# Gates of the forgetting branch ahead of its projections, and the output projection of two row blocks taken channel by channel behind the merges

## The chip, the cores and the metric

The kernel runs on one core of one Trainium2 chip. A core has TensorE (PE) for matrix products, VectorE (DVE), ScalarE (ACT) and GpSimd (POOL) for elementwise work, and SyncE (SP), whose queue issues nearly all the transfers here. The metric is the device time of one execution in microseconds; times given are medians of several runs. A profile is one execution taken by the hardware profiler. In it "PEld" is TensorE's loading of the stationary operand, which overlaps its products, and "L109" is line 109 of the kernel.

## What is computed

One decoder layer over 512 positions (T) of 1024 channels (D), in float32. An input u = x * (1 + scale) + shift is projected by one matrix into queries, keys and values of two attention branches of 8 heads each, into forget logits, and into two gates of 1024 channels. The part that the change touches is this, cut from the reference:

```
merged = jax.nn.sigmoid(g_a) * (y_fox @ w_fox_proj) + jax.nn.sigmoid(g_b) * (y_sb @ w_sb_proj)
attn_out = merged @ w_o
x = _layer_norm(DEEPNORM_ALPHA * x + (1.0 + gt1) * attn_out, ln1_g, ln1_b)
u2 = x * (1.0 + sc2) + sh2
h = _causal_depthwise_conv(u2 @ w_up, conv_w, conv_b)
```

g_a is the gate of the forgetting branch (FoX), g_b that of the stick-breaking branch. Behind it comes a gated MLP of width 2816 with its own layer norm.

## The kernel before

**Precision.** Each float32 operand is split into a high and a low part (names end in h and l: `hi_of` on ScalarE, `lo_of` on VectorE, line 77), and a product is three matmuls: high by high, high by low, low by high (`mm3`, lines 109 to 111). A matmul reads 128 rows against up to 512 columns.

**Weights.** All weight tiles (128 x 1024, 512 KB) stand in one list, `items`, in the order in which they are added. `weights(i, ahead)` issues the loads on SP's queue (line 125), up to item i + 3, into four buffers `raw`, and calls the processing of items up to i + `ahead` (2 unless said otherwise). `split_proc` splits a tile into `wh` and `wl`, three buffers of each. `ada_proc` turns a tile of the modulation matrix into one column of shift or scale (`mod_col`) on VectorE. `wo_proc` (line 573) multiplies a tile of w_o by (1 + gate), `gt[0]`, on GpSimd, then splits it in two halves into `woh` and `wol`, which stay in the pool `z` of 60 buffers.

**Order.** SP's queue keeps the order in which the program is written. On the other engines a scheduler orders the instructions: by its own model of their durations it issues what is ready, the one written first ahead of the others; on the chip each engine then works through its queue in that fixed order. The work that fills TensorE between the steps of the heads is a list, `stream`, of generators: projections of q, k and the gates (`proj`, 24 matmuls each), of the branches' outputs (`bproj`, 12 matmuls each). `fill(n)` takes n matmuls from it. Behind the last head `fill(1 << 30)` empties it.

**The merge.** `bproj(0, j)` multiplies the forgetting branch's output by columns j of its projection; VectorE multiplies the product by the sigmoid of gate j (line 568); `merge(j)` adds the other branch's share `ma[j]` on GpSimd (line 674) and splits the sum into `mh[j]` (ScalarE) and `ml[j]` (VectorE). `mh` and `ml` hold channels 128 j to 128 j + 127 of `merged`, transposed. j runs over the eight channel tiles (KT = 8).

In the list the order behind the heads is: `bproj(0, 0)`, a w_o tile, gate 3, `bproj(0, 1)`, a w_o tile, gate 4, and so on to gate 7; then `bproj` 5, 6 and 7; then the last three w_o tiles.

**The output projection.** `o_main(i)` (line 807) computes 128 rows of attn_out, in two halves e of 512 columns: 8 channels x 2 halves x 3 matmuls = 48, lines 817 to 819, into two PSUM banks (of eight). Then VectorE adds the residual `xn` (a load of x, line 813; add at 822) and normalizes (`ln_stats`). `o_turn(i)` transposes the block (line 836, eight transposes), scales it (lines 839 and 840) and splits it into `u2h` and `u2l`. The first three tiles of the up-projection (NSPLIT = 3) are multiplied with blocks 0 and 1 first (`up_mm` with 256 columns), then with blocks 2 and 3:

```
weights(last_wo, 0)
o_main(0)
o_main(1)
o_turn(0)
o_main(2)
o_turn(1)
o_main(3)
o_turn(2)
```

Of the kernel before, what the change touches and what calls it, by code (L numbers as in the profile page):

```python
# [8 lines left out]
F32 = mybir.dt.float32  # L9
# [7 lines left out]
P = 128  # L17
T = 512
D = 1024
KT = D // P  # L20
# [24 lines left out]
def layer_kernel(ctx: ExitStack, tc: tile.TileContext, out, xT, x, cT, crow, wa0, wa1, bcol, bgt, w1, wct, wv, bf,  # L45
                 wp, wo, lncol, lnrow, wup, cwb, wdn):
    nc = tc.nc
    ctx.enter_context(tc.manual_schedule(engines={nc.sync.engine}))
    V, S, G, PE = nc.vector, nc.scalar, nc.gpsimd, nc.tensor
# [10 lines left out]
    def nm(s):  # L60
        cnt[0] += 1
        return f"{s}_{cnt[0]}"

    def bank():
        return pp.tile([P, 512], F32, name=nm("ps"), tag="ps")
# [7 lines left out]
    def hi_of(o, i, scale=1.0):  # L73
        S.activation(o, i, AF.Copy, scale=scale)  # L74

    def lo_of(o, i, hi):
        return V.tensor_tensor(o, i, fl(hi), ALU.subtract)  # L77
# [27 lines left out]
    def z(dt, s, shape=(P, 512)):  # L105
        return zp.tile(list(shape), dt, name=nm(s), tag="z", bufs=NZ)
# [10 lines left out]
    def add_item(src, proc, cols=1024):  # L117
        items.append([src, proc, cols, None, None])
        return len(items) - 1

    def weights(i, ahead=AHEAD):
        while state["load"] < min(len(items), i + LOADS):
            it = items[state["load"]]
            it[3] = stg.tile([P, 1024], F32, name=nm("raw"), tag="raw", bufs=LOADS)
            nc.sync.dma_start(it[3][:, 0 : it[2]], it[0])
            state["load"] += 1
            while state["proc"] <= state["load"] - LOADS:
                process()
        while state["proc"] < min(len(items), i + 1 + ahead):
            process()  # L130
        return items[i][4]

    def process():
        it = items[state["proc"]]
        if state["proc"] < EARLY:
            with tc.issue_after(state["after"].ins):
                it[4] = it[1](it[3])
        else:
            it[4] = it[1](it[3])
        state["proc"] += 1  # L140
# [374 lines left out]
    def ada_proc(n):  # L515
        def f(r):
            if 8 <= n < 24:
                mod_col(2 + (n - 8) // 8, n % 8, r)
                return
            g, q = n // 4, n % 4  # L520
            if q == 0:
                ada_st[g] = z(F32, "ac2")
                V.tensor_scalar_mul(ada_st[g], r[:, 0:512], cTs[:, 0:1])
            acc = ada_st[g]
            for e in range(2):
                k = 2 * q + e
                if k > 0:
                    V.scalar_tensor_tensor(acc, r[:, e * 512 : (e + 1) * 512], cTs[:, k : k + 1], acc, ALU.mult, ALU.add)
        return f
# [24 lines left out]
    def gate_after(br, j):  # L554
        def f(ps):
            sg[(br, j)] = z(F32, "sg")
            S.activation(sg[(br, j)], ps, AF.Sigmoid)
        return f
# [12 lines left out]
    woh, wol = [], []  # L571
# [27 lines left out]
    stream, sums = [], []  # L599
    adas = [0]  # L600

    skip = [4]

    def add_ada(n=1):
        for _ in range(n):
            if skip[0]:
                skip[0] -= 1
            elif adas[0] < 24:
                add_item(wa1[adas[0]], ada_proc(adas[0]))
                adas[0] += 1  # L610
                if adas[0] in (4, 8):
                    stream.append((ada_split, (adas[0] // 4 - 1, len(items) - 1)))
                    sums.append([len(stream) + 1, adas[0] // 4 - 1])
# [4 lines left out]
    def add_proj(n, after):  # L618
        stream.append((proj, (add_item(wct[TILES.index(n)], split_proc), after)))
        flush_sum(len(stream))  # L620

    def flush_sum(n):
        if sums and n >= sums[0][0]:
            stream.append((ada_sum, (sums.pop(0)[1],)))
# [3 lines left out]
    def add_bproj(br, j, after):  # L628
        if j % 2 == 0:
            wpi[br] = add_item(wp[br, j // 2], split_proc)  # L630
        stream.append((bproj, (br, j, wpi[br], after)))
# [16 lines left out]
    def add_gate(br, j):  # L648
        add_proj(("sb" if br == 1 else "fox", j), gate_after(br, j))
        add_ada()  # L650
# [12 lines left out]
    for p in (5, 6, 7):  # L663
        add_pair(p)
        for _ in range(3):
            if bj:
                j = bj.pop(0)
                add_bproj(1, j, lambda m, j=j: ma.__setitem__(j, m))

    mh, ml = [], []  # L670

    def merge(j):
        def f(m):
            G.tensor_tensor(m, m, ma[j], ALU.add)
            a, b = z(F32R, "mh"), z(F32R, "ml")
            hi_of(a, m)
            lo_of(b, m, a)
            mh.append(a)
            ml.append(b)
        return f  # L680

    wos = [0]

    def add_wo():
        if wos[0] < KT:
            add_item(wo[wos[0]], wo_proc)
            wos[0] += 1

    for j in range(3):
        add_gate(0, j)  # L690
    marks["y0"] = len(stream)
    flush_sum(1 << 30)
    for j in range(KT):
        add_bproj(0, j, merge(j))
        if j < 5:
            add_wo()
        if j + 3 < KT:
            add_gate(0, j + 3)
    skip[0] = 0
    add_ada(24 - adas[0])  # L700
    while wos[0] < KT:
        add_wo()
    last_wo = len(items) - 1

    cur = {"n": 0, "g": None}
# [76 lines left out]
    def ln_stats(st):  # L782
        mv = cons.tile([P, 8], F32, name=nm("mv"), tag="mv", bufs=2)
        V.bn_aggr(mv[:, 0:2], st)
        v, s, y, t = mv[:, 2:3], mv[:, 3:4], mv[:, 4:5], mv[:, 5:6]
        S.activation(s, mv[:, 1:2], AF.Sqrt, bias=epsc)
        V.tensor_scalar_add(v, mv[:, 1:2], EPS)
        V.reciprocal(y, s)
        V.scalar_tensor_tensor(t, y, y, v, ALU.mult, ALU.mult)
        V.scalar_tensor_tensor(y, t, -3.0, y, ALU.add, ALU.mult)  # L790
        return mv[:, 0:1], y
# [13 lines left out]
    lnr = []  # L805

    def o_main(i):
        tb = slice(i * P, (i + 1) * P)
        xn = [z(F32, "xn") for _ in range(2)]
        st = cons.tile([P, 2, 6], F32, name=nm("st"), tag="st", bufs=2)  # L810
        ps2 = [bank(), bank()]
        for e in range(2):
            nc.sync.dma_start(xn[e], x[tb, e * 512 : (e + 1) * 512])
        cut = 6 if i == 0 else KT
        for e, ks in ((0, range(cut)), (1, range(cut)), (0, range(cut, KT)), (1, range(cut, KT))):
            for k in ks:
                PE.matmul(ps2[e], mh[k][:, tb], woh[k][e], start=k == 0, stop=False)  # L817
                PE.matmul(ps2[e], mh[k][:, tb], wol[k][e], start=False, stop=False)  # L818
                PE.matmul(ps2[e], ml[k][:, tb], woh[k][e], start=False, stop=k == KT - 1)  # L819
        for e in range(2):  # L820
            ps = ps2[e]
            V.scalar_tensor_tensor(xn[e], xn[e], ALPHA, ps, ALU.mult, ALU.add)
            V.bn_stats(st[:, e, :], xn[e])
        mu, rs = ln_stats(st)
        for e in range(2):
            V.tensor_scalar(xn[e], xn[e], mu, rs, ALU.subtract, ALU.mult)
        x1.append(xn)

    def o_turn(i):
        tb = slice(i * P, (i + 1) * P)  # L830
        xn = x1[i]
        pts = [bank(), bank()]
        ufs = [z(F32, "uf2"), z(F32, "uf2")]
        for e in range(2):
            for q in range(4):
                PE.transpose(pts[e][:, q * P : (q + 1) * P], xn[e][:, q * P : (q + 1) * P], ident)
        for q in range(4):
            c = slice(q * P, (q + 1) * P)
            S.activation(ufs[0][:, c], pts[0][:, c], AF.Identity, bias=bm[:, q : q + 1], scale=gm[:, q : q + 1])
            V.tensor_scalar(ufs[1][:, c], pts[1][:, c], gm[:, q + 4 : q + 5], bm[:, q + 4 : q + 5], ALU.mult, ALU.add)  # L840
        for e in range(2):
            uf = ufs[e].rearrange("p (a b) -> p a b", b=P)
            hi_of(u2h[:, 4 * e : 4 * e + 4, tb], uf)
            lo_of(u2l[:, 4 * e : 4 * e + 4, tb], uf, u2h[:, 4 * e : 4 * e + 4, tb])
# [23 lines left out]

    weights(last_wo, 0)
    o_main(0)  # L870
    o_main(1)
    o_turn(0)
    o_main(2)
    o_turn(1)
    o_main(3)
    o_turn(2)
    weights(wui[0], 0)
    bks = [bank() for n in range(NSPLIT)]
# [7 lines left out]
    for n in range(2 * FT):  # L886
        if n < NSPLIT:
            h, l = items[wui[n]][4]
            ps = bks[n]
            up_mm(ps, h, l, slice(256, 512))  # L890
        else:
            ps = bank()
# [49 lines left out]
    for i in range(NB):  # L942
        tb = slice(i * P, (i + 1) * P)
# [6 lines left out]
        for n, (e, c0, c1) in enumerate(pieces):  # L950
            sole = (i, e) == own
            ps = bank()[:, 0 : c1 - c0] if sole else acc[i][e]
# [87 lines left out]
```

## Time and profile before

| what | value |
|---|---|
| time, median of 3 runs | 780.85 us (780.64 to 781.18) |
| span of the profiled execution, first to last instruction | 779.4 us |
| runs' median above that span | 1.45 us |
| instructions | 9533 |
| TensorE clock granted, mean | 0.990 |
| moved to and from memory | 99.67 MB, mean 128 GB/s |

The profiled execution has no time of its own beside the span; what lies around the span is taken from the runs. The busy time of an engine is the time in which it executes something; a row of the timeline gives start, duration, engine, line, operation, output and inputs by the program's names, and in brackets the idle time before it and what ended it. In a row of the stretches (from:to) stand the length, then the busy time and number of instructions of PE, PEld, DVE, ACT and POOL, then the granted clock of TensorE (1.00 is full speed), the share of time in which the transfer engines were busy, and GB/s.

### The profile page before, as it was taken

The page shows a single profiled execution, that of the slowest core. Times are in us where ns is not written, and L with a number is a line of the kernel's source. Part 1 is how long each engine was busy: PE and PEld are TensorE (multiplying, and loading weights), DVE is VectorE, ACT ScalarE, POOL GpSimd, SP SyncE. Part 2 cuts the span into 40 slices and gives each one's busy share as a digit, 9 for nine tenths or more (in the row PEclk, how much of TensorE's full clock was granted, in tenths as well). Part 3 has the DMA queues.
Part 4 walks back from the last instruction along what each step waited for, and adds up shares of the span by engine and source line. Part 5 has one row for each costly group of instructions (what it writes and reads, how often), then busy time and mean ns, then how long its engine had stood idle before and what let it go on. Part 6 is the DMA issues. An engine that isn't in the chain of part 4 may idle for free.

```text
span 779.4 us, 9533 instructions
## 1 busy us (share of the span) xinstructions
PE 754.0 (97%) x3556; PEld 624.5 (80%) x3556; DVE 553.8 (71%) x854; ACT 350.6 (45%) x583; POOL 145.3 (19%) x106
## 2 busy tenths in 40 slices
PE   5998999999999999997999999999999999999995
PEld 3886887888888888885889888888888888888885
DVE  5979999967677876676546887777666665534666
ACT  3357686727567564344115434444444443222300
POOL 1020002000010012363000590000000043945500
PEclk9999999999999999999899999999999999999998
DMA  8951244452332423544301524353332314332302
GB/s 312 404 190 55 82 144 148 142 181 96 112 128 85 146 89 132 172 167 154 116 1 42 204 80 162 108 185 115 124 107 91 108 54 163 108 107 82 108 27 82
DMA packets 31104, 99.67 MB, mean 128 GB/s; under 512 B 4273, under 2 KB 4785, under 8 KB 31058
## 3 DMA queue, kind: packets, MB, share of 16 engines
q1 hardware_dynamic: 30546, 99.00, 36.4%
q8 instruction: 28, 0.46, 0.3%
q0 software_dynamic: 512, 0.07, 0.1%
q14 instruction: 18, 0.15, 0.1%
HBM read 96.88 MB, written 2.10 MB: 127 GB/s over the span
## 4 chain that ended last, share of the span: by engine, by line
PE 76%; DVE 8%; ACT 6%; DMA 5%; issue 3%; POOL 2%; SPq 0%; DVEq 0%; POOLq 0%; ACTq 0%
PE ps L109 14%; PE ps L110 14%; PE ps L111 14%; PE ps L253 6%; PE ps L932 5%; PE ps L931 5%; PE ps L933 5%; PE ps L817 2%; PE ps L494 2%; PE ps L476 2%; PE ps L818 2%; DMA raw<-in_wa 2%; PE ps L819 2%; ACT wh L74 1%; PE ps L419 1%
## 5 line engine op out<-in xcount | busy, mean ns | idle before, releaser
L77 DVE TENSOR_TENSOR wl<-raw,wh 128x1024 fp32r<-128x1024 f32 (+2 forms) x106 | 146.0, 1377 | 96.6 <-ACT wh L74 95.9
L74 ACT ACTIVATE wh<-raw 128x1024 fp32r<-128x1024 f32 (+2 forms) x106 | 110.3, 1041 | 109.1 <-PE ps L933 38.4
L109 PE MATMUL ps<-u2h,wh 128*128 128x512 f32 (+1 forms) x376 | 141.4, 376 | 0.0
L110 PE MATMUL ps<-u2l,wh 128*128 128x512 f32 (+1 forms) x376 | 141.3, 376 | 0.0
L111 PE MATMUL ps<-u2h,wl 128*128 128x512 f32 (+1 forms) x376 | 141.2, 376 | 0.0
L586 POOL TENSOR_TENSOR raw<-raw,gt 128x1024 f32<-128x1024 f32 x22 | 60.4, 2757 | 190.3 <-DVE gt L549 157.6
L109 PE MATMUL ps<-uh,wh 128*128 128x512 f32 x232 | 92.8, 400 | 0.0
L111 PE MATMUL ps<-uh,wl 128*128 128x512 f32 x232 | 90.9, 392 | 0.0
L110 PE MATMUL ps<-ul,wh 128*128 128x512 f32 x232 | 90.7, 391 | 0.0
L109 PEld LDWEIGHTS ps<-u2h,wh 128*128 128x128 f32 x376 | 70.8, 188 | 12.9
L111 PEld LDWEIGHTS ps<-u2h,wl 128*128 128x128 f32 x376 | 70.8, 188 | 12.8
L110 PEld LDWEIGHTS ps<-u2l,wh 128*128 128x128 f32 x376 | 70.8, 188 | 12.7
L111 PEld LDWEIGHTS ps<-uh,wl 128*128 128x128 f32 x232 | 43.6, 188 | 9.4
L109 PEld LDWEIGHTS ps<-uh,wh 128*128 128x128 f32 x232 | 43.6, 188 | 8.5 <-ACT pt L452 0.3
L110 PEld LDWEIGHTS ps<-ul,wh 128*128 128x128 f32 x232 | 43.7, 188 | 8.0
L932 PE MATMUL ps<-wl,hh 128*128 128x512 f32 x128 | 49.9, 390 | 0.0
L931 PE MATMUL ps<-wh,hh 128*128 128x512 f32 x128 | 49.8, 389 | 0.0
L933 PE MATMUL ps<-wh,hl 128*128 128x512 f32 x128 | 49.8, 389 | 0.0
L74 ACT ACTIVATE hh<-cv 128x512 fp32r<-128x512 f32 x22 | 13.9, 632 | 59.6 <-DVE cv L911 59.6
L910 ACT ACTIVATE cv<-cv 128x512 f32<-128x512 f32 x22 | 13.9, 632 | 54.5 <-DVE cv L905 54.5
L574 POOL TENSOR_TENSOR raw<-raw,gt 128x1024 f32<-128x1024 f32 x8 | 20.9, 2616 | 78.6 <-DVE m L77 42.2
L904 DVE SCALAR_TENSOR_TENSOR cv<-ps,cw,cv 128x511 f32<-128x511 f32 x44 | 32.7, 743 | 2.3 <-ACT cv L903 2.3
(188 smaller groups left out, 1446.9 us busy)
## 6 DMA issues: line engine op xcount, KB each, us to landing
raw<-in_wup SPq DMA_DIRECT2D x44, 512.0 KB, 3.3
raw<-in_wa SPq DMA_DIRECT2D x32, 512.0 KB, 3.3
raw<-in_wct SPq DMA_DIRECT2D x29, 512.0 KB, 3.3
raw<-in_wdn SPq DMA_DIRECT2D x22, 512.0 KB, 3.3
wa<-in_wa SPq DMA_DIRECT2D x14, 512.0 KB, 8.7
raw<-in_wp SPq DMA_DIRECT2D x8, 512.0 KB, 3.3
raw<-in_wo SPq DMA_DIRECT2D x8, 512.0 KB, 3.3
raw<-in_w SPq DMA_DIRECT2D x7, 452.0 KB, 8.3
```

Of the source, the lines that this page charges most:

```text
L74: S.activation(o, i, AF.Copy, scale=scale)
L77: return V.tensor_tensor(o, i, fl(hi), ALU.subtract)
L109: PE.matmul(ps, wh, ah, start=first, stop=False)
L110: PE.matmul(ps, wh, al, start=False, stop=False)
L111: PE.matmul(ps, wl, ah, start=False, stop=last)
L253: PE.matmul(grp[g], w, u, start=j == 0 and n == 0, stop=j == KT - 1 and n == (1 if g == 7 else 2))
L574: G.tensor_tensor(r, r, gt[0], ALU.mult)
L586: G.tensor_tensor(r, r, gt[1], ALU.mult)
L904: V.scalar_tensor_tensor(t[:, 1:], ps[:, 0:511], cw[:, n, 1:2], t[:, 1:], ALU.mult, ALU.add)
L931: PE.matmul(ps, hh[j][:, tb], w[0], start=first, stop=False)
L932: PE.matmul(ps, hh[j][:, tb], w[1], start=False, stop=False)
L933: PE.matmul(ps, hl[j][:, tb], w[0], start=False, stop=last)
```

## The change

Gates 3 to 7 are added to the list ahead of the first `bproj(0, j)`, with the modulation tiles that go with them. Each w_o tile but the last is added one `bproj` later than the `bproj` of its channel. Row blocks 0 and 1 of the output projection leave `o_main`: `o_part(k)` adds channel k to both halves of both blocks (12 matmuls) and stands in the list behind `bproj(0, k + 2)`, the last two behind `bproj(0, 7)`. Their four PSUM banks, `acc2`, are taken at `o_part(0)` and held until `o_main(0)` and `o_main(1)`, of which only the residual and the normalization are left. `o_main(2)` and `o_main(3)` keep their matmuls, one half after the other. `o_main(2)` now stands ahead of `o_turn(0)`, `o_main(3)` ahead of `o_turn(1)`.

```
--- before.py
+++ after.py
@@ -679,27 +679,47 @@
             ml.append(b)
         return f
 
-    wos = [0]
-
-    def add_wo():
-        if wos[0] < KT:
-            add_item(wo[wos[0]], wo_proc)
-            wos[0] += 1
+    wps2, acc2 = [], []
+
+    def x_tiles(i):
+        tb = slice(i * P, (i + 1) * P)
+        xn = [z(F32, "xn") for _ in range(2)]
+        for e in range(2):
+            nc.sync.dma_start(xn[e], x[tb, e * 512 : (e + 1) * 512])
+        return xn
+
+    def o_step(ps, i, e, k):
+        tb = slice(i * P, (i + 1) * P)
+        PE.matmul(ps, mh[k][:, tb], woh[k][e], start=k == 0, stop=False)
+        PE.matmul(ps, mh[k][:, tb], wol[k][e], start=False, stop=False)
+        PE.matmul(ps, ml[k][:, tb], woh[k][e], start=False, stop=k == KT - 1)
+
+    def o_part(k):
+        if k == 0:
+            acc2.extend([bank(), bank()] for _ in range(2))
+        weights(wps2[k], 0)
+        for i in range(2):
+            for e in range(2):
+                o_step(acc2[i][e], i, e, k)
+            yield 6
 
     for j in range(3):
         add_gate(0, j)
     marks["y0"] = len(stream)
     flush_sum(1 << 30)
+    for j in range(3, KT):
+        add_gate(0, j)
+    skip[0] = 0
+    add_ada(24 - adas[0])
     for j in range(KT):
         add_bproj(0, j, merge(j))
-        if j < 5:
-            add_wo()
-        if j + 3 < KT:
-            add_gate(0, j + 3)
-    skip[0] = 0
-    add_ada(24 - adas[0])
-    while wos[0] < KT:
-        add_wo()
+        if j:
+            wps2.append(add_item(wo[j - 1], wo_proc))
+            if j > 1:
+                stream.append((o_part, (j - 2,)))
+    wps2.append(add_item(wo[KT - 1], wo_proc))
+    for k in (KT - 2, KT - 1):
+        stream.append((o_part, (k,)))
     last_wo = len(items) - 1
 
     cur = {"n": 0, "g": None}
@@ -805,18 +825,13 @@
     lnr = []
 
     def o_main(i):
-        tb = slice(i * P, (i + 1) * P)
-        xn = [z(F32, "xn") for _ in range(2)]
         st = cons.tile([P, 2, 6], F32, name=nm("st"), tag="st", bufs=2)
-        ps2 = [bank(), bank()]
-        for e in range(2):
-            nc.sync.dma_start(xn[e], x[tb, e * 512 : (e + 1) * 512])
-        cut = 6 if i == 0 else KT
-        for e, ks in ((0, range(cut)), (1, range(cut)), (0, range(cut, KT)), (1, range(cut, KT))):
-            for k in ks:
-                PE.matmul(ps2[e], mh[k][:, tb], woh[k][e], start=k == 0, stop=False)
-                PE.matmul(ps2[e], mh[k][:, tb], wol[k][e], start=False, stop=False)
-                PE.matmul(ps2[e], ml[k][:, tb], woh[k][e], start=False, stop=k == KT - 1)
+        xn = x_tiles(i)
+        ps2 = acc2[i] if i < 2 else [bank(), bank()]
+        if i > 1:
+            for e in range(2):
+                for k in range(KT):
+                    o_step(ps2[e], i, e, k)
         for e in range(2):
             ps = ps2[e]
             V.scalar_tensor_tensor(xn[e], xn[e], ALPHA, ps, ALU.mult, ALU.add)
@@ -869,10 +884,10 @@
     weights(last_wo, 0)
     o_main(0)
     o_main(1)
+    o_main(2)
     o_turn(0)
-    o_main(2)
+    o_main(3)
     o_turn(1)
-    o_main(3)
     o_turn(2)
     weights(wui[0], 0)
     bks = [bank() for n in range(NSPLIT)]
```

## The prediction

> **What bounds the kernel now.** I read the page's first two parts, then TensorE's waits, then its timeline from the last attention head to the first matmul of the up-projection.
>
> ```profile
> span 779.4 us, 9533 instructions
> PE 754.0 (97%) x3556; PEld 624.5 (80%) x3556; DVE 553.8 (71%) x854; ACT 350.6 (45%) x583; POOL 145.3 (19%) x106
> PEclk9999999999999999999899999999999999999998
> ```
>
> TensorE is busy for 97% of the span, so time can come only from its gaps and from stretches at a lower clock. One slice of PEclk in the middle reads 8. The timeline of TensorE around it (start, duration, engine, line, operation; in brackets the idle time before and what ended it):
>
> ```profile
> 305.47 0.40 PE L109 MATMUL ps<-yh,wh 128*128 128x512 f32 x1
> ...
> 354.60 0.39 PE L817 MATMUL ps<-woh,mh 128*128 128x512 f32 x1
> ...
> 357.78 0.39 PE L819 MATMUL ps<-woh,ml 128*128 128x512 f32 x1
> 358.77 0.50 PE L817 MATMUL ps<-woh,mh 128*128 128x512 f32 x1 [0.60 <-ACT mh L74]
> 359.10 0.40 PE L818 MATMUL ps<-wol,mh 128*128 128x512 f32 x1
> 360.11 0.50 PE L819 MATMUL ps<-woh,ml 128*128 128x512 f32 x1 [0.61 <-DVE ml L77]
> ...
> 365.02 0.39 PE L819 MATMUL ps<-woh,ml 128*128 128x512 f32 x1
> 368.48 0.79 PE L817 MATMUL ps<-woh,mh 128*128 128x512 f32 x1 [3.07 <-ACT woh L74]
> ...
> 375.16 0.40 PE L817 MATMUL ps<-woh,mh 128*128 128x512 f32 x1
> ```
>
> From 305.47 to 354.60 stand 216 matmuls (96 of bproj, 120 of gates 3 to 7), 0.227 us from start to start. Against that pace the wait for mh costs 358.77 - 357.78 - 0.23 = 0.76 us, the one for ml 360.11 - 359.10 - 0.23 = 0.78, the one for the last channel 368.48 - 365.02 - 0.23 = 3.23. Then come 15 matmuls in 6.68 us (368.48 to 375.16) that take 3.41 at the full pace: 3.27 more. The stretches show why (length, busy us of PE, PEld, DVE, ACT, POOL, then the granted clock):
>
> ```profile
> 358.00:360.00 2.00, 0.90 (x3) 0.30 (x2) 1.77 (x3) 1.76 (x4) 0.00 (x0) 1.00 0.84 259
> ...
> 366.00:368.00 2.00, 0.00 (x0) 0.00 (x0) 0.19 (x2) 0.72 (x2) 1.24 (x1) 1.00 0.00 0
> 368.00:370.00 2.00, 1.51 (x3) 0.91 (x4) 1.83 (x3) 1.98 (x3) 0.00 (x0) 0.50 0.49 158
> ```
>
> Behind the long wait the clock was 0.50, behind the short ones 1.00. All four together: 0.76 + 0.78 + 3.23 + 3.27 = **8.04 us**, and from 375.16 on TensorE is full until the tail. Who was late there, by the chain of work that ended last:
>
> ```profile
> 353.80 3.25 DMA raw<-in_wup
> ...
> 358.23 1.23 DVE wl L77
> ...
> 364.31 0.69 DVE sg L568
> ...
> 367.27 0.63 ACT mh L74
> ```
>
> bproj 7, the last, was through on TensorE at 354.60. Its product with the gate (DVE, L568) began only at 364.31, 9.7 us late: VectorE, in order, stood behind wl of an up-projection tile whose load landed at 357, and behind wol. Its merge (mh at 367.27), with the last woh behind it on ACT, is what the output projection waits for.
>
> **The change, part by part.** *TensorE's work* is the same: 120 gate matmuls, 96 of bproj, and for blocks 0 and 1 the same 96 L817 to L819 matmuls in another order, each adding into one of four banks. Moved ahead, the five gates run 305.5 to 332.7 (120 x 0.227); then come 8 bproj and 8 o_part of 12 matmuls (2.72 us) each, to 376.2. Those four banks leave four for bproj, whose bank is free once L568 has read it; late by 3 bproj (8.2 us) costs nothing.
>
> *Merges.* One merge and one w_o tile cost (count, shortest/median/longest ns):
>
> ```profile
> L674 POOL TENSOR_TENSOR sg<-sg,sg x8: 1287/1296/2204, 312.2 to 365.1; 128x512 f32<-128x512 f32 x8
> L77 DVE TENSOR_TENSOR ml<-sg,mh x8: 684/692/2885, 314.2 to 367.9; 128x512 fp32r<-128x512 f32 x8
> L574 POOL TENSOR_TENSOR raw<-raw,gt x8: 2393/2404/3146, 274.3 to 349.5; 128x1024 f32<-128x1024 f32 x8
> L77 DVE TENSOR_TENSOR wol<-raw,woh x16: 675/683/2886, 308.3 to 369.1; 128x512 fp32r<-128x512 f32 x16
> ```
>
> A merge undisturbed takes 0.69 + 1.30 + 0.63 + 0.69 = 3.3 us after its bproj. Between bproj k and o_part k lie two units of 2.72 us (5.4 us) for k = 0 and 7, three (8.2) for 1 and 6, four (10.9) for 2 to 5. So undisturbed no o_part waits, and the 8.04 us go. The merges are disturbed, though, by POOL's products:
>
> ```profile
> 293.43 3.15 POOL L574 TENSOR_TENSOR raw<-raw,gt 128x1024 f32<-128x1024 f32 x1 [16.70 <-DMA raw<-in_wo]
> 295.05 0.69 DVE L501 TENSOR_TENSOR yf<-ps,ytmp 64x512 f32<-64x512 f32 x1 [0.73 <-ACT ytmp L500]
> ...
> 344.05 3.49 DVE L77 TENSOR_TENSOR wol<-raw,woh 128x512 fp32r<-128x512 f32 x2
> 344.16 2.83 POOL L574 TENSOR_TENSOR raw<-raw,gt 128x1024 f32<-128x1024 f32 x1 [1.72 <-DVE wl L77]
> ```
>
> Two wol (1.37 alone) took 3.49 beside a POOL product, L501 with one input in PSUM kept its 0.69. So POOL and the DVE operations that read two SBUF tiles take turns: 2.40 + 1.37 = 3.77 us a w_o tile, 1.30 + 0.69 = 1.99 a merge, 1.23 a weight tile's wl. How full that path was before, by the groups of VectorE and POOL from 309.8 to 368.6 (58.8 us):
>
> ```profile
> L77 DVE TENSOR_TENSOR wl<-raw,wh 128x1024 fp32r<-128x1024 f32 x9 | 13.0, 1445 | 3.2 <-ACT wh L74 3.0
> ...
> L164 DVE SCALAR_TENSOR_TENSOR raw<-raw,cbc 128x1024 f32<-128x1024 f32 x2 | 2.4, 1220 | 1.5 <-DMA raw<-in_wa 1.5
> ...
> L574 POOL TENSOR_TENSOR raw<-raw,gt 128x1024 f32<-128x1024 f32 x6 | 15.4, 2565 | 19.7 <-DVE wol L77 13.2 <-DMA raw<-in_wo 2.8 <-ACT woh L74 1.9
> ```
>
> At undisturbed durations that is 6 x 3.77 + 8 merges x 1.99 + 9 x 1.23 + 2.4 = 52 us, 88% full. After, all eight w_o tiles lie behind gate 7 in the load order. The chain shows when the first can come:
>
> ```profile
> 303.98 1.24 DVE wl L77
> ...
> 305.23 4.34 DMA raw<-in_wo
> ...
> 309.81 2.40 POOL raw L574
> ```
>
> The split at 303.98 frees a raw buffer; of the other three, after the change, gates 6 and 7 and the first projection tile hold one each, since they wait for one of three wh buffers. So the first w_o product runs at about 310, when before the third did. From there to the last ml near 372 are 62 us for 8 x 3.77 + 8 x 1.99 + 8 wl (9.8) + one modulation product (1.2) = 57 us, 92%. If the work fits, the cost is nothing; at the 88% of before it takes 64.9 us, 2.9 late. I take **0.9 us**, nearer to none, since the products start under 27 us of gates; a wait of 3 us would also bring the low clock back.
>
> *Loads.* With three wh buffers a gate's split runs two gates (10.9 us) ahead of its use, so running five back to back costs nothing; uncovered, it would be a load each:
>
> ```profile
> raw<-in_wct SPq DMA_DIRECT2D x29, 512.0 KB, 3.3
> ```
>
> In SP's queue the first three w_up loads now pass those of lnc and cw; these are needed by o_turn(0), over 10 us later. The x tiles keep their place behind the w_up loads and are needed from about 375 on; late, they would cost their own landing. Blocks 0 and 1 now finish 1.4 us apart, and their normalizations stand in one row on DVE under the 10.9 us of o_main(2), when o_turn(0) needs only the first of them.
>
> *o_turn(1)* is the part that costs. Before, o_main(3) stood between it and up_mm. Now o_main(3), o_turn(1), o_turn(2) and the first up_mm, which reads blocks 0 and 1, follow each other. How long a transposed block takes, from o_turn(0), which also ran right behind an o_main:
>
> ```profile
> 384.70 1.03 PE L836 MATMUL ps<-ident,xn 128*128 128x128 f32 x8
> 385.34 1.50 ACT L839 ACTIVATE uf<-ps,bm,gm 128x128 f32<-128x128 f32 x4 [10.25 <-PE ps L836]
> 385.49 0.48 PE L817 MATMUL ps<-woh,mh 128*128 128x512 f32 x1
> ...
> 386.98 0.61 ACT L74 ACTIVATE u2h<-uf 128x512 fp32r<-128x512 f32 x1
> ...
> 388.14 0.69 DVE L77 TENSOR_TENSOR u2l<-uf,u2h 128x512 fp32r<-128x512 f32 x1
> ...
> 389.66 0.69 DVE L77 TENSOR_TENSOR u2l<-uf,u2h 128x512 fp32r<-128x512 f32 x1
> ```
>
> The first half of u2h is there 2.9 us behind the first transpose (387.59), the first half of u2l 4.1 us (388.83), the second 5.65 (390.35). TensorE arrives after two turns of 0.79, at 1.6. It waits 1.3 for the first matmul, 1.1 for the second, about 0.2 in the middle: 2.6, and some 0.1 for o_turn(2)'s evacuations in the same queues: **2.7 us**. Bounds: 0 if the scheduler puts o_turn(1) ahead of o_main(3), 2.6 + 1.5 (four ACT evacuations of o_turn(2) ahead) = 4.1.
>
> Sum: 8.04 - 0.9 - 2.7 = 4.44 us, span 775.0. The runs lie 1.45 us above the profiled span (780.85 against 779.4), so **776.4 us**. The runs alone, 780.64 to 781.18, would tell 0.2% (1.56 us) from no change.
>
> **Rivals.** (a) The last merges are late again: the w_o work runs as thin as before, o_part 6 or 7 waits about 3.2 us and the clock falls for 3.3 more. For it: 92% full, and queues in fixed order. Against: nothing but merges and wl is left at the end, with 5.4 to 8.2 us of room. 8.04 - 6.5 - 2.7 = -1.2: 782.0, or down to 779.5 where the wait stays short of the clock's fall.
>
> (b) Slower: POOL and DVE pace the o_parts. If no more than the first w_o tile is ready by 332.7 (the others held behind the projection tiles in the raw buffers), 7 x 3.77 + 15.9 + 5 x 1.23 = 48.5 us of turns, at 88% 55, face the 40.8 us of TensorE up to o_part 7: 14 us of waits, less 5.3: 789.7. It decides from 5.3 us of waits on (8.04 - 2.7). Against: before, the first w_o product ran at 274, 30 us ahead of bproj 0.
>
> (c) o_turn(1) is moved forward or hidden and no merge waits: 780.85 - 8.04 = 772.8 to 774.
>
> (d) The 2.7 us at up_mm let the clock fall: up to 3.3 more, 779.7. Here 0.6 us waits left it at 1.00, 3.07 us did not; 2.7 in two pieces lies near the latter. The Trainium skill (TensorE: Matmul & The Clock Gate, Part 1) has the clock halved after an idle window of about 3.4 us; by that rule neither 2.7 nor the 3.07 us seen here would suffice, so the trace disagrees, and the rule alone would give this case no chance.
>
> (e) The scheduler, which orders by readiness, puts bproj or o_main(2) ahead of o_parts so that little changes: 780.85.
>
> **How the numbers follow.** The forecast 0.53 (775 to 778.5), (a) 0.14, (b) 0.07, (c) 0.14, (d) 0.10, (e) 0.02. Faster takes the forecast, (c) and half of (d): 0.72 and a little of (a), 0.74; slower (b) and a fifth of (a), 0.10; same the rest, 0.16. The range 773.0 to 780.8 leaves out part of (c) and what is above in (a) and (b).
>
> **What would show it.** Right: no wait of TensorE over 1 us between 305 and 398 us, the clock 1.00 there, the eight w_o products on POOL from about 310 on, a wait of L109 and L110 of 2 to 3 us just behind o_turn(2), at about 400 us. Wrong: a wait of o_step's matmuls for woh, mh or ml over 2 us; a clock under 1 in this stretch; up_mm starting without a wait; o_main(2) finding x tiles missing.

## The result, and the profile after

The changed kernel takes 786.62 us (median; 785.52 to 787.67) against 780.85 us before. The ratio is 1.0072, with a 95% interval of 1.0059 to 1.0084: slower by 5.8 us. The profiled execution spans 785.0 us against 779.4, 5.6 more. The forecast was 776.4 us and the range ended at 780.8; both are missed.

The first two parts of the page of the changed kernel:

```profile
span 785.0 us, 9527 instructions
PE 755.5 (96%) x3556; PEld 624.6 (80%) x3556; DVE 555.9 (71%) x854; ACT 350.9 (45%) x583; POOL 144.5 (18%) x106
PEclk9998999999999999999999999999999999999998
```

TensorE executes the same 3556 matmuls, busy for 755.5 us against 754.0, 1.5 of the 5.6 us. The dip of the clock in the middle of the span no longer fills a slice; one near 75 us does (it is the subject of the last section). The rest is idle time of TensorE. Its timeline shows where, from the first matmul of `bproj(0, 0)` to the first of the up-projection:

```profile
333.47 0.39 PE L109 MATMUL ps<-yh,wh 128*128 128x512 f32 x1
...
341.86 0.39 PE L694 MATMUL ps<-wol,mh 128*128 128x512 f32 x1
343.69 0.50 PE L695 MATMUL ps<-woh,ml 128*128 128x512 f32 x1 [1.44 <-DVE ml L77]
...
366.09 0.40 PE L694 MATMUL ps<-wol,mh 128*128 128x512 f32 x1
367.97 0.50 PE L695 MATMUL ps<-woh,ml 128*128 128x512 f32 x1 [1.48 <-DVE ml L77]
...
375.62 0.39 PE L695 MATMUL ps<-woh,ml 128*128 128x512 f32 x1
378.52 0.50 PE L693 MATMUL ps<-woh,mh 128*128 128x512 f32 x1 [2.51 <-ACT mh L74]
...
381.42 0.39 PE L695 MATMUL ps<-woh,ml 128*128 128x512 f32 x1
383.30 0.50 PE L693 MATMUL ps<-woh,mh 128*128 128x512 f32 x1 [1.50 <-ACT woh L74]
...
414.25 0.50 PE L109 MATMUL ps<-u2h,wh 128*128 128x256 f32 x2 [1.33 <-ACT u2h L74]
414.97 0.39 PE L110 MATMUL ps<-u2l,wh 128*128 128x256 f32 x1 [0.22 <-DVE u2l L77]
```

L693 to L695 are now the three matmuls of `o_step`. Against the pace of 0.23 us from start to start, the four waits cost 343.69 - 341.86 - 0.23 = 1.60 us at `o_part(0)`, 367.97 - 366.09 - 0.23 = 1.65 at `o_part(4)`, 378.52 - 375.62 - 0.23 = 2.67 at `o_part(6)` and 383.30 - 381.42 - 0.23 = 1.65 at `o_part(7)`: 7.6 us. Losses under 0.6 us each behind them and a stretch at half clock after the last add 3.7, which makes 11.3 us between 333.47 and 387.9. The waits ahead of `up_mm` add 2.3. Together that is 13.6 us; before, the same reckoning over the whole stretch gave 8.9 us. So up_mm begins at 414.25 instead of 409.05, 5.2 us later: 0.77 of it is older, since the last head's L476, which stands ahead of everything that the change touches, began at 300.47 instead of 299.70; the other 4.4 are, to 0.3 us, these losses less those of before. The remainder of the span adds 0.4.

The stretches show the clock (length, busy us of PE, PEld, DVE, ACT, POOL, the clock, DMA share, GB/s):

```profile
378.00:380.00 2.00, 1.48 (x5) 0.97 (x6) 1.50 (x3) 1.42 (x2) 0.13 (x1) 1.00 0.41 130
...
385.00:386.00 1.00, 1.00 (x4) 0.81 (x3) 0.69 (x1) 0.07 (x1) 0.00 (x0) 0.50 0.95 287
```

Behind the longest wait (2.67 us) it stayed at 1.00; behind the last (1.65 us) it was 0.50.

Why the merges were late starts 25 us earlier, under the gates. The timeline of GpSimd, the products of w_o with 1 + gate:

```profile
309.34 2.39 POOL L574 TENSOR_TENSOR raw<-raw,gt 128x1024 f32<-128x1024 f32 x1 [76.42 <-DMA raw<-in_wo]
322.95 2.40 POOL L574 TENSOR_TENSOR raw<-raw,gt 128x1024 f32<-128x1024 f32 x1 [11.22 <-DMA raw<-in_wo]
329.89 2.70 POOL L574 TENSOR_TENSOR raw<-raw,gt 128x1024 f32<-128x1024 f32 x1 [4.53 <-DMA raw<-in_wo]
```

The first product runs at 309.34, but the second only 13.6 us later, waiting for its load. The waits of SP's queue from 300 to 400 us (who waited for whom: us in all, times, longest) say what the loads waited for:

```profile
SPq L125 <- DVE wl L77: 35.3, 8, 7.7
SPq L125 <- DVE wol L77: 27.2, 7, 13.6
```

A load needs a free `raw` buffer, and a buffer is freed when its tile is split. While the gates run, one gate or projection tile is split per gate, since its split needs one of three `wh` buffers and TensorE frees one per 24 matmuls (5.4 us). ScalarE's first and fourth of four such splits in a row, 16.27 us apart, show this pace; the last row is the first split of a w_o tile:

```profile
311.74 1.06 ACT L74 ACTIVATE wh<-raw 128x1024 fp32r<-128x1024 f32 x1 [3.31 <-PE ps L110]
...
328.01 1.06 ACT L74 ACTIVATE wh<-raw 128x1024 fp32r<-128x1024 f32 x1 [3.84 <-PE ps L110]
...
329.45 1.14 ACT L74 ACTIVATE woh<-raw 128x512 fp32r<-128x512 f32 x2
```

A w_o tile needs no `wh`. But the first one, whose product ended at 311.73, has its `woh` in ScalarE's queue behind all four of these splits, so it kept its `raw` buffer until its two wol were done at 333.74 (row below). Without the product on GpSimd (an experiment below) this `woh` runs at 329.79, just as late: the place in the queue holds it, not the product. Why the scheduler put it there is not shown. So few w_o tiles are touched while the gates run: all of them now stand behind the last gate in the list, they get what buffers the gate and projection tiles leave, and they give them back late. The stretch of gates 3 to 7, after and then before:

```profile
305.00:333.00 28.00, 28.00 (x127) 23.31 (x126) 12.03 (x9) 9.25 (x14) 7.50 (x3) 1.00 0.29 94
```

```profile
305.00:333.00 28.00, 28.00 (x125) 22.96 (x125) 18.79 (x27) 11.77 (x20) 8.94 (x6) 1.00 0.55 185
```

TensorE is full in both. VectorE is busy for 12.03 us instead of 18.79, and the transfers move 94 GB/s instead of 185. The w_o work that lay there falls into the next 50 us, where the merges are. The groups of VectorE and GpSimd from 333.5 to 383.5 us:

```profile
L77 DVE TENSOR_TENSOR wol<-raw,woh 128x512 fp32r<-128x512 f32 x14 | 14.3, 1076 | 0.0
L77 DVE TENSOR_TENSOR ml<-sg,mh 128x512 fp32r<-128x512 f32 x8 | 8.5, 1063 | 14.0 <-ACT mh L74 14.0
L77 DVE TENSOR_TENSOR wl<-raw,wh 128x1024 fp32r<-128x1024 f32 x5 | 6.1, 1220 | 3.1 <-ACT wh L74 3.1
L674 POOL TENSOR_TENSOR sg<-sg,sg 128x512 f32<-128x512 f32 x8 | 13.4, 1675 | 16.3 <-DVE sg L568 16.3
L574 POOL TENSOR_TENSOR raw<-raw,gt 128x1024 f32<-128x1024 f32 x5 | 12.9, 2572 | 7.0 <-DVE sg L568 4.5 <-DMA raw<-in_wo 2.0 <-issue 0.5
```

Fourteen of sixteen wol and five of eight products are still to be done there. At the undisturbed durations that the prediction used, this is 14 x 0.685 + 5 x 2.40 + 8 merges x 1.99 + 5 x 1.23 = 43.7 us of turns in 50 us, 87% full, as full as the path was before (88%). The first two wol, and then one merge of those, on VectorE:

```profile
330.24 3.50 DVE L77 TENSOR_TENSOR wol<-raw,woh 128x512 fp32r<-128x512 f32 x2
...
356.16 6.91 DVE L77 TENSOR_TENSOR wol<-raw,woh 128x512 fp32r<-128x512 f32 x4
362.99 0.68 DVE L568 TENSOR_TENSOR sg<-ps,sg 128x512 f32<-128x512 f32 x1
365.73 2.18 DVE L77 TENSOR_TENSOR ml<-sg,mh 128x512 fp32r<-128x512 f32 x1 [2.07 <-ACT mh L74]
```

`bproj(0, 4)` was through on TensorE at 354.6; its L568 ran at 362.99, behind four wol that took 6.91 us where four alone take 2.7. Then its ml took 2.18 us instead of 0.69. GpSimd at the same time:

```profile
355.72 2.78 POOL L574 TENSOR_TENSOR raw<-raw,gt 128x1024 f32<-128x1024 f32 x1 [2.05 <-DMA raw<-in_wo]
358.98 2.94 POOL L574 TENSOR_TENSOR raw<-raw,gt 128x1024 f32<-128x1024 f32 x1 [0.48 <-issue]
...
364.99 2.38 POOL L574 TENSOR_TENSOR raw<-raw,gt 128x1024 f32<-128x1024 f32 x1
```

The products of 355.72 and 358.98 fall on the four wol, the one of 364.99 ends at 367.37 inside the ml, and `o_part(4)` starts its L695 at 367.97, when that ml is done. What looks like a slow operation of VectorE is, by these times, one that waits for GpSimd's turn to end.

By the Trainium skill (SBUF — State Buffer, "SBUF: two separate sides") a VectorE operation with two inputs in SBUF and a GpSimd operation that reads SBUF hold a shared pair of ports exclusively, the other one blocking for the whole instruction. The traces agree: ml took 2.18 us beside a product and 0.69 elsewhere, while L501 of the profile before, which has one input in PSUM, kept 0.69 beside one (295.05, in the prediction). No L568 of the changed kernel fell beside a product.

### The profile page after: what moved, and what is told of

The parts are those of the page before. It is cut to its first block, busy times and chain, and to the rows that moved or that the text cites. A ratio compares the mean times of both kernels' runs of the same rounds, so it can differ in the third digit from the quotient of the medians.

```text
span 785.0 us, 9527 instructions
## 1 busy us (share of the span) xinstructions
PE 755.5 (96%) x3556; PEld 624.6 (80%) x3556; DVE 555.9 (71%) x854; ACT 350.9 (45%) x583; POOL 144.5 (18%) x106
## 4 chain that ended last, share of the span: by engine, by line
PE 82%; DVE 6%; ACT 5%; issue 2%; DMA 2%; POOL 2%; SPq 0%; DVEq 0%; POOLq 0%; ACTq 0%
PE ps L109 16%; PE ps L110 16%; PE ps L111 16%; PE ps L253 6%; PE ps L948 5%; PE ps L946 5%; PE ps L947 5%; PE ps L494 2%; PE ps L476 2%; PE ps L419 1%; POOL sg L674 1%; ACT wh L74 1%; PE ps L420 1%; PE ps L694 1%; PE ps L695 1%
## 5 line engine op out<-in xcount | busy, mean ns | idle before, releaser
L109 PE MATMUL ps<-u2h,wh 128*128 128x512 f32 (+1 forms) x376 | 141.2, 376 | 1.3 <-ACT u2h L74 1.3
L110 PE MATMUL ps<-u2l,wh 128*128 128x512 f32 (+1 forms) x376 | 141.3, 376 | 0.2 <-DVE u2l L77 0.2
L109 PE MATMUL ps<-uh,wh 128*128 128x512 f32 x232 | 93.0, 401 | 0.0
L110 PE MATMUL ps<-ul,wh 128*128 128x512 f32 x232 | 90.8, 392 | 0.0
L109 PEld LDWEIGHTS ps<-u2h,wh 128*128 128x128 f32 x376 | 70.7, 188 | 14.3 <-ACT u2h L74 1.6
L110 PEld LDWEIGHTS ps<-u2l,wh 128*128 128x128 f32 x376 | 70.8, 188 | 13.1 <-DVE u2l L77 0.4
L111 PEld LDWEIGHTS ps<-uh,wl 128*128 128x128 f32 x232 | 43.7, 188 | 9.4
L109 PEld LDWEIGHTS ps<-uh,wh 128*128 128x128 f32 x232 | 43.8, 189 | 8.5 <-ACT pt L452 0.3
L110 PEld LDWEIGHTS ps<-ul,wh 128*128 128x128 f32 x232 | 43.9, 189 | 8.0
L947 PE MATMUL ps<-wl,hh 128*128 128x512 f32 x128 | 49.8, 389 | 0.0
L948 PE MATMUL ps<-wh,hl 128*128 128x512 f32 x128 | 49.8, 389 | 0.0
L946 PE MATMUL ps<-wh,hh 128*128 128x512 f32 x128 | 49.8, 389 | 0.0
```

Of the source, the lines that this page charges most:

```text
L109: PE.matmul(ps, wh, ah, start=first, stop=False)
L110: PE.matmul(ps, wh, al, start=False, stop=False)
L111: PE.matmul(ps, wl, ah, start=False, stop=last)
L946: PE.matmul(ps, hh[j][:, tb], w[0], start=first, stop=False)
L947: PE.matmul(ps, hh[j][:, tb], w[1], start=False, stop=False)
L948: PE.matmul(ps, hl[j][:, tb], w[0], start=False, stop=last)
```

## The experiments

Three theories were set against each other. A: the elementwise work of w_o, moved out of the gates' stretch into that of the projections, delays the merges. B: the channel-by-channel order itself, which needs each merge soon, costs the time. C: the loads, pressed together behind the gates, set the pace. The losses given below are counted as above: starts of TensorE's matmuls against their full pace between 300 and 430 us, clock included (before 8.9 us, after 13.6).

### w_o tiles 0 to 3 under the gates

All else as in the changed kernel; four w_o tiles stand behind gates 3 to 6 in the list again.

```
     for j in range(3, KT):
         add_gate(0, j)
+        if j < KT - 1:
+            wps2.append(add_item(wo[j - 3], wo_proc))
...
         add_bproj(0, j, merge(j))
-        if j:
+        if j > 4:
             wps2.append(add_item(wo[j - 1], wo_proc))
-            if j > 1:
-                stream.append((o_part, (j - 2,)))
+        if j > 1:
+            stream.append((o_part, (j - 2,)))
```

> The changed kernel with one thing moved: w_o tiles 0 to 3 are added behind gates 3 to 6 instead of behind bproj 1 to 4. Theory A (the elementwise work of the w_o tiles has been moved out of the stretch of the gates, where VectorE and GpSimd now stand idle, into that of bproj and o_part, where it stands in fixed queues ahead of the merges and takes turns with them): four products run before bproj 0, the merges come in time, and of the 11 us lost to waits and the low clock between bproj 0 and o_main(2) some 7 go: 778 to 781 us. Theory B (the channelwise order of the output projection itself costs: it needs each merge sooner, whatever else is queued): waits stay at 9 us or more, 784 to 787. Theory C (w_o tiles are loaded too late, the raw buffers are the bound): the loads come earlier, so this too gets faster, 779 to 782; it does not tell C from A.

Measured: 776.02 us (773.62 to 779.70), ratio to before 0.9939 (0.9920 to 0.9958). Better than A expected. The stretch from 305 to 333 us in this kernel, and the one row of TensorE's waits that names its o_step:

```profile
305.00:333.00 28.00, 28.00 (x125) 23.17 (x125) 17.14 (x17) 12.16 (x19) 9.68 (x4) 1.00 0.55 181
```

```profile
PE ps L694 <- DVE wol L77: 0.3, 1, 0.3
```

VectorE is at 17.14 us and the transfers at 181 GB/s again, and of the o_parts' waits 0.3 us is left. The loss is 3.4 us, of which 2.3 is the wait at up_mm (1.3 and 0.2 us by its rows, 2.3 against the pace). The place of four tiles in the list decides over about 10 us. B falls, since the channel-by-channel order is here too. A fits, but so does C, since these tiles are loaded earlier too; the product's experiments below tell the two apart.

### The gates ahead, without the channel-by-channel order

```
-            if j > 1:
-                stream.append((o_part, (j - 2,)))
...
-        ps2 = acc2[i] if i < 2 else [bank(), bank()]
-        if i > 1:
-            for e in range(2):
-                for k in range(KT):
-                    o_step(ps2[e], i, e, k)
+        ps2 = [bank(), bank()]
+        cut = 6 if i == 0 else KT
+        for e, ks in ((0, range(cut)), (1, range(cut)), (0, range(cut, KT)), (1, range(cut, KT))):
+            for k in ks:
+                o_step(ps2[e], i, e, k)
...
-    o_main(2)
     o_turn(0)
-    o_main(3)
+    o_main(2)
     o_turn(1)
+    o_main(3)
```

> Half of the change alone: gates 3 to 7 ahead of the bproj and the w_o tiles behind them as in the changed kernel, but no o_part; o_main 0 and 1 with their own matmuls and the turns in their old places. Theory A: the merges and w_o tiles are done at about 380 us of the span as in the changed kernel, but TensorE has only the eight bproj (21.8 us) to fill the time with, so it waits in o_main(0) for 10 to 20 us, part of it at half the clock: 788 to 796. Theory B: without the channelwise order the loss is that of before, 779 to 782. Theory C: as A.

Measured: 790.93 us (789.63 to 791.92), ratio 1.0130 (1.0109 to 1.0151), worse than the whole change and inside what A gave. The two longest waits of TensorE in the stretch, by the view of its waits:

```profile
PE ps L109 <- ACT wh L74: 5.7, 1, 5.7
...
PE ps L694 <- DVE wol L77: 2.2, 2, 1.7
```

Without o_parts between them, the projections themselves run into the w_o work: ScalarE, in order, has the split of a projection's tile (wh) behind an mh, and this mh waits for an add of GpSimd, which waits for L568, which stands on VectorE behind four wol (346.3 to 349.9 us). The timeline of ScalarE:

```profile
352.25 0.63 ACT L74 ACTIVATE mh<-sg 128x512 fp32r<-128x512 f32 x1 [3.44 <-POOL sg L674]
352.79 0.61 ACT L74 ACTIVATE woh<-raw 128x512 fp32r<-128x512 f32 x1
353.31 1.04 ACT L74 ACTIVATE wh<-raw 128x1024 fp32r<-128x1024 f32 x1
```

TensorE started no matmul between 348.3 and 354.4. The gates ahead, with all w_o tiles behind them, are the half of the change that costs: 790.93 - 781.02 = 9.9 us without the o_parts, and 786.62 - 776.37 = 10.2 with them (776.37 is the next experiment).

### The channel-by-channel order, without the gates ahead

```
-    for j in range(3, KT):
-        add_gate(0, j)
-    skip[0] = 0
-    add_ada(24 - adas[0])
     for j in range(KT):
         add_bproj(0, j, merge(j))
-        if j:
-            wps2.append(add_item(wo[j - 1], wo_proc))
-            if j > 1:
-                stream.append((o_part, (j - 2,)))
-    wps2.append(add_item(wo[KT - 1], wo_proc))
+        if j < 5:
+            wps2.append(add_item(wo[j], wo_proc))
+        if j + 3 < KT:
+            add_gate(0, j + 3)
+        if j > 1:
+            stream.append((o_part, (j - 2,)))
+    skip[0] = 0
+    add_ada(24 - adas[0])
+    while len(wps2) < KT:
+        wps2.append(add_item(wo[len(wps2)], wo_proc))
```

> The other half alone: gates and w_o tiles in their old places (bproj j, w_o tile j, gate j + 3), blocks 0 and 1 channelwise with o_part k behind bproj k + 2, the new order of o_main and o_turn. Theory A: the merges keep the pace of before, which was late only for the last three, and TensorE now has o_parts to do meanwhile: waits of 2 to 4 us with o_part 6 and 7, plus 2.3 at up_mm that the changed kernel shows: 776 to 780. Theory B: the waits are those of the changed kernel, 784 to 787. Theory C: the loads come in the order of before: 776 to 780.

Measured: 776.37 us (774.73 to 779.19), ratio 0.9944 (0.9927 to 0.9961), as A expected. One wait at `o_part(7)` (1.65 us against the pace, with half clock behind it in the profiled execution) and the one at up_mm are left; the loss is 6.8 us. So the order that the change brings is worth 4.6 us (781.02, the median of before in these runs, less 776.37), and the gates ahead with the w_o tiles behind them turn this into a loss. The gates ahead with four w_o tiles among them cost nothing next to this kernel (776.02). B is out.

### Without the product on GpSimd

The result leaves out the factor 1 + gate of w_o; loads, splits and matmuls are all there.

```
     def wo_proc(r):
-        G.tensor_tensor(r, r, gt[0], ALU.mult)
```

> The changed kernel without the product of the w_o tiles with (1 + gate) on GpSimd: that factor is left out of the result. Loads, splits, merges and their order of writing stay. Theory A: eight products of 2.4 us and what they block on VectorE are gone, the waits fall by 6 to 9 us: 777.5 to 780.5. Theory C: the loads come through the same four buffers as late as before, at most 2 to 3 us better: 783.5 to 785. Theory B: 784 to 787.

Measured: 776.99 us (776.08 to 777.22), ratio 0.9945 (0.9930 to 0.9961); a little better than A's bounds and far from C's. The waits of the o_parts shrink to 0.5 and 0.3 us with every load at its place in the queue. The first two w_o loads and the projection tile between them even come 0.3 us later than in the changed kernel (the first at 306.34 instead of 306.00). The later ones come earlier, as their buffers are free sooner (the first w_up load at 354.58 instead of 363.13). The loads follow the elementwise work and do not set the pace: C is out. By the medians the eight products of 2.4 us cost the changed kernel 9.6 us.

### The product on VectorE

If the products hurt, is it because they fill an engine, or because the two engines block each other and a product stands ahead of the merge's add?

```
     def wo_proc(r):
-        G.tensor_tensor(r, r, gt[0], ALU.mult)
+        V.tensor_tensor(r, r, gt[0], ALU.mult)
```

> The changed kernel with the product of the w_o tiles with (1 + gate) on VectorE instead of GpSimd, same place in the program. It takes about 1.23 us there (as wl, two inputs in SBUF) instead of 2.4, and nothing of GpSimd blocks VectorE but the eight additions of the merges. Theory A1 (GpSimd's products and VectorE taking turns is what makes the merges late): eight times 2.4 us of turns become eight times 1.23, the waits fall by 4 to 8 us: 779 to 783. Theory A2 (it is VectorE's own queue: merges stand behind whatever has been put ahead of them): VectorE has 9.8 us more to do in the stretch where the merges are late, 787 to 792.

Measured: 780.17 us (778.66 to 781.10), ratio 0.9993 (0.9980 to 1.0006): A1 holds, A2 falls. The groups of VectorE from 332 to 382 us:

```profile
L77 DVE TENSOR_TENSOR wol<-raw,woh 128x512 fp32r<-128x512 f32 x14 | 9.9, 761 | 0.0
L77 DVE TENSOR_TENSOR ml<-sg,mh 128x512 fp32r<-128x512 f32 x8 | 6.2, 773 | 8.0 <-ACT mh L74 8.0
...
L574 DVE TENSOR_TENSOR raw<-raw,gt 128x1024 f32<-128x1024 f32 x5 | 6.1, 1217 | 0.0
```

VectorE does five products more, 6.1 us, and yet is busy for slightly less: wol fell from 14.3 to 9.9 us, ml from 8.5 to 6.2, 6.7 us together. A product on GpSimd costs 2.4 us of the common turns, on VectorE 1.22. The stretch is still too full for the o_parts (waits of 0.78 and 1.65 us), as the tiles are as late as in the changed kernel.

### o_turn(1) ahead of o_main(3)

```
     o_turn(0)
-    o_main(3)
     o_turn(1)
+    o_main(3)
     o_turn(2)
```

> The changed kernel with o_turn(1) ahead of o_main(3); nothing else moved. In the changed kernel TensorE waits at the first up_mm for u2h and u2l of block 1: 1.67 us and 0.48 us above its pace. Theory A (o_turn(1) had its evacuation hidden under o_main(3), and the new order took that cover): the waits go, 2.2 us: 784.4 us, 784 to 785. Rival D (VectorE is in arrears from the late merges, so the waits only move to o_turn(1) or to o_main(3)): 786 to 787.

Measured: 783.79 us (782.69 to 785.45), ratio 1.0040 (1.0024 to 1.0055), as expected. The waits of L109 and L110 at up_mm are gone, those of the o_parts stand (1.65, 1.66, 2.65 and 1.65 us against the pace). The term of o_turn(1) is thus measured by itself: 786.62 - 783.79 = 2.8 us by the medians; by the ratios, each to its own runs of before, 1.0072 - 1.0040 of 780.85 is 2.5 us.

### The same behind the two better kernels

The same swap of two lines, once in the kernel with the channel-by-channel order alone, once in the one with w_o tiles under the gates.

> The channelwise output projection with the gates and w_o tiles in their old places, and o_turn(1) ahead of o_main(3). Theory A: 2.2 us below the same kernel without this move (776.4): 774.2, 773 to 775.5. Rival D: 776 to 777.

> Gates ahead, w_o tiles 0 to 3 behind gates 3 to 6, and o_turn(1) ahead of o_main(3). Theory A: 2.2 us below the same kernel without this move (776.0): 773.8, 772.5 to 775. It leaves no wait of TensorE above 0.6 us between the last head and the up-projection. Rival D: 776.

Measured: 774.09 us (772.32 to 774.65), ratio 0.9910 (0.9885 to 0.9935), for the first, and 775.00 us (773.83 to 775.67), ratio 0.9924 (0.9900 to 0.9948), for the second; the first lies in the middle of what was expected, the second at the upper edge. By the medians the swap is worth 2.3 us in the first and only 1.0 in the second, where 2.2 was expected; in the profiled executions of the second the loss falls from 3.4 to 1.4 us, so the smaller figure can be the spread of its runs. The intervals overlap; which of the two is better stays open. Both beat the kernel before and the changed one. In the first, no wait of TensorE is left between 305 us and the up-projection; of the five that its span holds, these are the first and the last:

```profile
PE ps L253 <- ACT uh L226: 6.2, 1, 6.2
...
PE ps L419 <- ACT m L74: 0.4, 2, 0.2
```

All five (the others are for L476, L156 and L420) lie ahead of the stretch, and its loss between 300 and 430 us is 0.5 us.

## Why the prediction was wrong

**The step that failed** is the term "I take **0.9 us**", and in it the sum over the 62 us from the first product on, "8 x 3.77 + 8 x 1.99 + 8 wl (9.8)". In place of 0.9 us the trace has 11.3 between 333.47 and 387.9. The first product did run at 309.34, where about 310 was predicted. But the 62 us were counted from it as if the others could follow at once. The step that reasoned out which tiles hold the four `raw` buffers was applied to the first w_o tile only. Applied to the next ones it would have given a buffer per gate (5.4 us), which goes to the next tile of the list: of the five loads from 306.00 to 330.35, three are w_o tiles and two projection tiles. The sum takes for granted besides that a w_o tile gives its buffer back soon after its product; the first kept it until 333.74, since its `woh` stood behind four other splits in ScalarE's queue. How much each of the two delays costs, no run here shows. Three products run before `bproj(0, 0)`, and one of the eight tiles has its wol.

**Rival (b) had the mechanism and the formula, with a count that was off by two products.** It put seven w_o tiles behind 332.7 and came to 14 us of waits; seven tiles' wol were left indeed, but only five products. With what was left at 333.5 (43.7 us of turns, from the groups above) its rule gives 43.7 / 0.88 = 49.6 us against 40.8 us of TensorE up to `o_part(7)`: 8.8 us. Measured from `bproj(0, 0)` to `o_part(7)`: 383.30 - 333.47 = 49.8, so 9.0 us. It was given 0.07. The argument against it ("before, the first w_o product ran at 274, 30 us ahead of bproj 0") spoke of the very lead that the change takes away. With the 2.3 us lost behind `o_part(7)`'s wait, nearly all to the clock, the prediction's own sum gives 8.04 - 8.8 - 2.3 - 2.7 = -5.8 and 786.6 us. That this is the measured time to the tenth is luck in part: 43.7 and 2.3 are taken from the trace after the fact, 2.7 is 0.4 too large, and 0.77 us of the real difference are older than the change.

**Rival (a)** came true as part of it: o_part 6 and 7 waited 2.67 and 1.65 us, and the clock fell behind the second. Its 6.5 us agree with the 6.6 found there by luck: it had 3.2 of waits and 3.3 of clock, the trace 4.3 and 2.3. What it missed are the waits at o_part 0 and 4, which come from the same crowd, not from the end of the line.

**Right were:** the gates without a wait (333.47 for 332.7, and 0.77 of it older than the change); the order of the bprojs and o_parts, as the list has it, so that (e) fell; the taking of turns of GpSimd and VectorE; no harm from the loads moved past lnc, cw and the x tiles, as `o_main(2)` began without a wait; the old 8.04 us being gone wherever the merges are in time, which the kernel without a wait shows (its 774.09 us lies just above the 772.8 to 774 that (c) gave for that case).

**o_turn(1)** was predicted at 2.7 us and measured at 1.67 for the first matmul of up_mm, 0.48 for the second and 0.11 behind it: 2.3 us. The mechanism was right and the term 0.4 us too large. The first half of u2h was there 3.2 us behind the first transpose instead of 2.9, the first half of u2l 3.9 instead of 4.1. So the wait for the first matmul was larger than the 1.3 predicted, and the one for the second much smaller than the 1.1.

**(d)** did not happen in the profiled execution of the changed kernel: the clock was 1.00 behind up_mm's wait. The "3 us" at which the prediction has the low clock come back are no threshold, though, as the last section shows.

## What to carry to other kernels

When work is moved ahead in a list that feeds a few buffers, ask not when the first of the displaced tiles arrives but at what rate the rest can: here one buffer per 5.4 us gate, shared with other tiles, so that a 28 us head start was worth three products and one finished tile of eight. Ask too in which engine's queue a tile's last step stands, since until then it keeps its buffer. A stretch that fills TensorE is also the room in which the other engines do later work; emptying it of elementwise work shows no cost there and sends the bill to the next stretch. Where GpSimd and VectorE take turns, count their durations as one sum, and count a product where it is cheapest (1.22 us on VectorE, 2.4 on GpSimd).

## What the runs showed of the hardware that was not expected

**The same wait may or may not halve the clock.** At `o_part(7)` TensorE waited 1.65 us against the pace in four kernels' profiles (after, the order alone, the product on VectorE, o_turn(1) ahead). In the first two half clock followed, in the last two none. The wait at up_mm (1.66 and 0.49) is alike in five profiles (after, w_o under the gates, the order alone, without the product, the product on VectorE); only with the product on VectorE did half clock follow:

```profile
405.28 0.50 PE L109 MATMUL ps<-u2h,wh 128*128 128x256 f32 x2 [1.33 <-ACT u2h L74]
```

```profile
406.00:407.00 1.00, 0.99 (x6) 0.99 (x7) 1.00 (x4) 0.97 (x4) 0.00 (x0) 0.74 0.00 0
407.00:408.00 1.00, 1.00 (x7) 1.00 (x6) 1.00 (x3) 0.46 (x1) 0.00 (x0) 0.50 0.00 0
408.00:409.00 1.00, 1.00 (x6) 1.00 (x6) 1.00 (x4) 0.15 (x1) 0.00 (x0) 0.50 0.00 0
409.00:410.00 1.00, 1.00 (x7) 1.00 (x6) 0.90 (x2) 0.48 (x1) 0.00 (x0) 0.55 0.00 0
```

The lost clock is 0.26 + 0.50 + 0.50 + 0.45 = 1.7 us, or 3.4 us at half; it cost 1.5 us of matmuls (20 that take 2.4 us at 0.12 each took 3.89, from 406.23 to 410.12). And a wait of 2.67 us (after, at 375.62) left the clock at 1.00. The wait for L476 near 74 us, which no kernel here changes, gave all three outcomes. After, and then w_o under the gates:

```profile
74.19 0.87 PE L476 MATMUL ps<-ident,pt 128*128 128x128 f32 x3 [3.27 <-DVE m L77]
```

```profile
74.00:76.00 2.00, 1.81 (x8) 1.75 (x9) 1.97 (x6) 1.95 (x6) 0.00 (x0) 0.50 0.84 258
...
78.00:80.00 2.00, 2.00 (x11) 2.00 (x11) 2.00 (x5) 2.00 (x6) 0.00 (x0) 0.50 0.24 31
```

```profile
73.59 0.52 PE L476 MATMUL ps<-ident,pt 128*128 128x128 f32 x3 [3.27 <-DVE m L77]
```

```profile
74.00:76.00 2.00, 2.00 (x16) 1.67 (x16) 1.95 (x5) 2.00 (x5) 0.00 (x0) 1.00 0.54 207
```

The same 3.27 us led to about 6.8 us at half clock in the one and to none in the other; of the other eight profiles, two show 6.8 us and six, the one before among them, about 3.4. If TensorE is full meanwhile, 6.8 us at half speed cost 3.4, and 3.4 cost 1.7. Such draws are part of the spread of one kernel: the seven runs with w_o under the gates reach from 773.62 us (mean clock 0.998) to 779.70 (0.991). They can also explain the 0.77 us at 300 us, which no step of the change touches; that was not tested by itself.

The Trainium skill (TensorE: Matmul & The Clock Gate, Part 1) has the clock decided over windows of about 3.4 us that run freely and don't start anew with the kernel. The stretches of 3.4 and 6.8 us, and the outcome that changes from run to run, agree with that. Its condition, at least one idle window, does not fit as a length of one wait: here half clock followed a wait of 1.65 us twice, and did not follow one of 2.67 us. What else a window counts, no run here shows.
